# V turned by VectorE and stored in 128-byte runs, and one Strassen product added onto another's bank in the next quad

## The chip, the cores and the metric

One core of a Trainium2 chip runs the whole program. The metric is the device time of one execution in microseconds (us); the median of the runs counts. The engines are named as the profile names them: PE (TensorE, matrix products), PEld (its weight loads), DVE (VectorE), ACT (ScalarE), POOL (GpSimd) and SP (SyncE, which here issues nearly all DMAs, strictly in the order of the program).

## The reference

A decoder block of 2048 positions and width 1024, in float32. One combined projection feeds two branches:

```python
proj = x @ w_in[l] + b_in[l]                      # (2048, 1024) @ (1024, 9216)
q, k, v, g_attn, u_lru, g_lru, gate_logits = jnp.split(proj, SPLIT_POINTS, axis=-1)
...                                               # rotary q and k, three dilated band attentions
attn = jnp.sum(wts[..., None] * jnp.stack(outs, axis=0), axis=0)
attn = attn.reshape(B, S, ATTN_OUT_WIDTH).astype(dt) * jax.nn.silu(g_attn)
y_a = attn @ w_attn_proj[l]
...                                               # convolution, gated linear recurrence -> h
y_b = (h * jax.nn.silu(g_lru)) @ w_lru_proj[l]
merged = gates[:, :, 0] * y_a + gates[:, :, 1] * y_b
out = merged @ w_out[l] + b_out[l]
x = layer_norm(DEEPNORM_ALPHA * x + out, ln_gain[l], ln_bias[l])
```

The projection's 9216 columns are 72 tiles of 128: 12 each of q, k and v, 4 of the attention gate, 8 each of the recurrence's input and gate, 16 of merge gates.

## The kernel before

The kernel has three stages. The first, about two thirds of the time, is the projection; the second the attention; the third the output projections and the norm. The change is in the first.

**Quads and products.** The first stage works in quads: two column tiles (f0, f1) of the weights against two chunks of 512 positions (c0, c1), once for each half of the sequence, so 36 quads per half and 72 in all (`plan`, line 556). Results lie with the feature on the partition and the position along the row. Each operand is split into a high and a low float32r part, and a product of 128x512 with depth 512 takes 4 x 3 = 12 matmuls (`product`, line 607). The first quad of a half is computed plainly with 8 products; all others by Strassen's scheme with seven products P1 to P7, whose weights (A11, A12, A22, S1 to S4) and position blocks (B11, B21, B22, T1 to T4) are sums of quarters. The order of the products is written out by hand on line 122: MID for 66 quads, EDGE and FIRST for the last and the second of a half.

**Ticks.** The program is written out tick by tick: one tick is one product on PE (12 matmuls), and `where` (line 926) lists the ticks. In each tick the main loop first issues the product; then come the events due in this tick (weight loads, sums and the preparation of high and low weight parts: lines 680 to 705), then the chains, then `evacuate` (line 633), which takes the product's PSUM bank and forms results. Weights of quad s are prepared from `t0` on, which is 4 ticks ahead of the quad in the first half and 3 in the second, where low parts are loaded again from DRAM (`load_lo`, line 284) that the first half has stored there (`wl_scr`).

**Strassen sums.** `evacuate` keeps running sums in SBUF: `e` is P1, `u2` = P1 - P6, `u3` = u2 + P7. After P5 DVE forms the result for (f1, c1) and then adds P5 to `u2` (the profile's `u<-u,q`), to which P3 is added at the end for (f0, c1). The results of f1 come out with their sign turned (`sgn` = -1), and each later step corrects that. Products use four PSUM banks of tag `q`; two are used for the transposes (`t`), two for the gates of the recurrence (`g`).

**Chains.** A result starts a chain, a generator that goes on by one step when the tick, a free slot of the 32 SBUF slots and the estimated budget of the engines allow it (`run_chains`, line 187). `qk_chain` (line 299) does the rotation; it copies its tile with rows exchanged by four DMAs (`sw<-y`), and for the third dilation group stores q in runs of 128 bytes (line 341). `silu_chain` (line 398) makes the gates. `v_chain` (line 351) brings V to DRAM with the position on the row, as the attention reads it: PE turns the tile in four transposes of 128x128 into a PSUM bank (`vtp`, line 358), in the middle of a product; ACT copies the bank to one of two tiles `vs` and corrects the sign (line 366); and SP stores it with one DMA of 256 KB in runs of 512 bytes (line 370). There are 12 V tiles and 4 chunks, so 48 such chains; their transposes lie between 105 and 382 us and between 819 and 1100 us.

Of the kernel before, what the change touches and what calls it, by code (L numbers as in the profile page):

```python
# [31 lines left out]
def hybrid_block_kernel(ctx: ExitStack, tc: tile.TileContext, a: dict, out: bass.AP):  # L32
# [315 lines left out]
    vs_free = [sl_p.tile([P, 4, P], F32, name=f"vs{j}") for j in range(2)]  # L348
    tog = {"n": 0}

    def v_chain(vt, sgn, f, c):
        g, hp = divmod(f - FT_V, 4)
        st = {}

        def turn():
            tp = st["tp"] = ps.tile([P, 4, P], F32, tag="t", name=f"vtp{f}_{c}", bufs=2)
            for b in range(4):
                pe.transpose(tp[:, b, :], flat(vt)[:, b * P:(b + 1) * P], ident)  # L358
            give(vt)

        yield Ask(cond=lambda: tog["n"] < 2)
        tog["n"] += 1
        pe_later(2, turn)
        yield Ask(lag=3, cond=lambda: len(vs_free) > 0, ACT=.66)
        vs = vs_free.pop(0)
        act.activation(vs, st["tp"], AF.Copy, scale=sgn)
        tog["n"] -= 1
        yield Ask()
        dst = v_scr[g][hp // 2][c * CH:(c + 1) * CH, (hp % 2) * P:(hp % 2) * P + P]
        sp.dma_start(dst.rearrange("(b p) f -> p b f", p=P), vs)  # L370
        vs_free.append(vs)
# [26 lines left out]
    def silu_chain(y, sgn, f, c):  # L398
# [3 lines left out]
        act.activation(y, y, AF.Identity, scale=0.25 * sgn, bias=bq[:, f:f + 1])  # L402
# [157 lines left out]
    ticks = [8 if pl[2] is None else 7 for pl in plan]  # L560
    base = [sum(ticks[:s]) for s in range(NQ + 1)]
# [45 lines left out]
    def product(s, j):  # L607
# [6 lines left out]
        if first:  # L614
            Q["b"] = ps.tile([P, CH], F32, tag="q", name=f"q{j}_{s}", bufs=4)
        bank = Q["b"]
        h, l = U[s, n]
        i = 0
        for kk in range(4):
            ks = slice(kk * P, (kk + 1) * P)  # L620
            for w, xx in ((h, 0), (h, 1), (l, 0)):
                pe.matmul(bank, w[:, ks], x[:, kk, xx], start=(first and i == 0), stop=(last and i == 11))  # L622
                i += 1
            if i == 6:
                run(pe_late)
# [7 lines left out]
    def evacuate(s, j):  # L633
        half, _, order, _, _ = plan[s]
        b = Q["b"]
        c0, c1 = 2 * half, 2 * half + 1
        if order is None:
            fi, k, c = PLAIN[j]
            if k:
                result(s, fi, c0 + c, b, None)  # L640
            return
        pid = order[j]
        if pid == 1:
# [10 lines left out]
        elif pid == 5:  # L654
            result(s, 1, c1, b, Q["u3"])
            tt(dve, Q["u2"], Q["u2"], b, ALU.add)
# [3 lines left out]
        elif pid == 4:  # L660
            result(s, 1, c0, b, Q["u3"])
        elif order.index(5) > j:
            Q["p3"] = take(f"p{s}", F32)
            act.activation(Q["p3"], b, AF.Copy)
        else:
            result(s, 0, c1, b, Q["u2"])
        last = {"e": (2, 6), "u2": (3, 5), "u3": (4, 5), "p3": (5,)}
        for n, p in last.items():
            if n in Q and pid in p and all(order.index(x) <= j for x in p):
# [3 lines left out]
    COST = {1: dict(ACT=.66), 2: dict(DVE=.72), 6: dict(DVE=.72), 7: dict(DVE=.72), 5: dict(DVE=1.45), 4: dict(DVE=.72), 3: dict(DVE=.72)}  # L673
# [7 lines left out]
    for s in range(1, NQ):  # L681
# [20 lines left out]
        for j in range(7):  # L702
            if plan[s][0] and j % 2 == 0:
                at(t0 + j - 1, lambda s=s, j=j: load_lo(s, j))
            at(t0 + j, lambda s=s, j=j: prep_w(s, j))
# [220 lines left out]
    where = [(s, j) for s in range(NQ) for j in range(ticks[s])]  # L926
    for T, (s, j) in enumerate(where):
# [10 lines left out]
        if s == NQ - 1:  # L938
            for fn in ((), first[:2], first[2:], second[:2], firstv, second[2:], ())[j]:
# [652 lines left out]
```

## Time and profile before

| | |
|---|---|
| runs, us | 2103.63, 2104.59, 2108.65; median 2104.59 |
| profiled execution: its span, first to last instruction | 2101.9 us (its own device time isn't listed beside it) |
| PE busy | 2086.3 us, 99% of the span |
| DVE, ACT, POOL busy | 1662.7, 1116.7, 493.1 us |
| mean granted TensorE clock | 0.999 |
| first stage | to about 1440 us |
| time of DMA packets on the queue of SP (q1) | 70.5% of 16 engines |

The profile is of one execution. "Busy" is the time in which an engine had an instruction of a group running; matmuls are pipelined, so that their rows overlap, and a busy PE need not be PE at its peak. A row of a group gives line, engine and operation, out<-in, the tiles' shapes and the count, then busy time, mean ns of one, and the idle time ahead of it with what ended it. In a row of a stretch (from:to) stand the length, the busy time of each engine with its number of instructions, the granted clock, and the DMA engines' share and GB/s. SPq is SP's queue of DMA issues; the time of an issue is SP's own, and "to landing" goes from the issue until the data has arrived.

### The profile page before, as it was taken

Reading aid. Unit: us, or ns where it says so; the run is one execution under the profiler, and the core shown is the slowest. Engines: PE = TensorE matmul, PEld = TensorE weight load, DVE = VectorE, ACT = ScalarE, POOL = GpSimd, SP = SyncE. Lnnn points to the kernel's source line nnn. Section 1 sums busy time; section 2 is a strip of 40 time slices with the busy share of each in tenths; the row PEclk is TensorE's granted clock in tenths of the full one; section 3 lists DMA queues with packets and bytes.
Section 4 is the critical chain, followed back from the end, with each engine's and each line's share of the span. In section 5 each row is a group of like instructions: output and inputs, shape, how many; then the busy total and the mean of one; then the engine's idle time right before and its main releaser. Section 6 shows DMA issues by size and latency. Waiting matters only on the chain.

```text
span 2101.9 us, 35814 instructions
## 1 busy us (share of the span) xinstructions
PE 2086.3 (99%) x12016; PEld 1726.9 (82%) x12016; DVE 1662.7 (79%) x3179; ACT 1116.7 (53%) x2341; POOL 493.1 (23%) x468
## 2 busy tenths in 40 slices
PE   8999999999999999999999999999999999999998
PEld 7888888888888888888888888888999888888887
DVE  8987888889988867787877888877999645576667
ACT  6455456457457565666666775766999411211100
POOL 1111111110111011231221222222545344431120
PEclk9999999999999999999999999999999999999999
DMA  8987997987997967777779778769996788864432
GB/s 271 276 261 225 274 285 216 282 283 235 278 294 242 332 208 204 231 227 220 225 254 278 254 252 266 252 219 374 355 359 236 228 296 281 298 224 160 154 105 71
DMA packets 327160, 524.69 MB, mean 250 GB/s; under 512 B 105536, under 2 KB 135232, under 8 KB 323136
## 3 DMA queue, kind: packets, MB, share of 16 engines
q1 hardware_dynamic: 307088, 489.54, 70.5%
q0 software_dynamic: 12256, 19.42, 5.5%
q10 hardware_dynamic: 7632, 13.44, 1.7%
q8 instruction: 96, 1.57, 0.3%
q14 instruction: 88, 0.72, 0.1%
HBM read 317.14 MB, written 190.45 MB: 241 GB/s over the span
## 4 chain that ended last, share of the span: by engine, by line
PE 91%; DVE 3%; DMA 3%; ACT 2%; issue 1%; SPq 0%; DVEq 0%; ACTq 0%
PE q L622 66%; PE yb L1340 3%; PE yb L1341 3%; PE z L1451 3%; PE yb L1342 3%; PE z L1450 3%; PE z L1452 3%; ACT p L1023 2%; DVE p L1015 2%; PE ya L1419 1%; PE ya L1418 1%; PE ya L1420 1%; PE g L492 1%; PE vtp L358 1%; DMA B<-k_scr 1%; DMA o_scr<-ot 1%
## 5 line engine op out<-in xcount | busy, mean ns | idle before, releaser
L622 PE MATMUL q<-xT,hS 128*128 128x512 f32 x1680 | 521.0, 391 | 0.0
L622 PE MATMUL q<-xT,l 128*128 128x512 f32 x1120 | 436.0, 389 | 0.0
L622 PE MATMUL q<-xB,hA 128*128 128x512 f32 x1248 | 388.9, 393 | 6.0 <-ACT xB L215 6.0
L622 PEld LDWEIGHTS q<-xT,hS 128*128 128x128 f32 x1680 | 312.9, 188 | 69.0 <-issue 5.5
L622 PE MATMUL q<-xB,l 128*128 128x512 f32 x904 | 352.9, 390 | 0.0
L622 PEld LDWEIGHTS q<-xB,hA 128*128 128x128 f32 x1248 | 233.8, 189 | 57.3 <-ACT xB L215 6.0
L622 PEld LDWEIGHTS q<-xT,l 128*128 128x128 f32 x1120 | 210.2, 188 | 44.1
L622 PEld LDWEIGHTS q<-xB,l 128*128 128x128 f32 x904 | 170.3, 188 | 36.0
L245 POOL DMA_DIRECT2D wS<-in_w_in_dram x70 | 61.9, 950 | 491.5 <-DMA wS<-in_w_in_dram 140.0
L622 PE MATMUL q<-xB,hS 128*128 128x512 f32 x560 | 174.0, 392 | 0.0
L1023 ACT ACTIVATE p<-p,sta 128x256 f32<-128x256 f32 (+1 forms) x384 | 172.7, 469 | 1.2 <-PE pt L1034 0.8
L622 PE MATMUL q<-xT,hA 128*128 128x512 f32 x560 | 173.0, 390 | 0.0
L269 ACT ACTIVATE hA<-wA 128x512 fp32r<-128x512 f32 x218 | 134.9, 623 | 54.4 <-DMA wA<-in_w_in_dram 24.9
L269 ACT ACTIVATE hS<-S 128x512 fp32r<-128x512 f32 x175 | 109.0, 623 | 79.3 <-DVE S L227 49.0
L227 POOL TENSOR_TENSOR S<-S,wA 128x512 f32<-128x512 f32 x35 | 45.5, 1301 | 391.8 <-DVE S L227 208.8
L622 PEld LDWEIGHTS q<-xT,hA 128*128 128x128 f32 x560 | 104.7, 188 | 23.0 <-issue 1.5
L622 PEld LDWEIGHTS q<-xB,hS 128*128 128x128 f32 x560 | 104.0, 188 | 22.4 <-issue 1.5
L1015 DVE CUSTOM_DVE_ANT_0 p<-s,mask 128x256 f32<-128x256 f32 (+1 forms) x384 | 116.4, 360 | 0.2 <-PE s L1008 0.2
L1451 PE MATMUL z<-wo,mh 128*128 128x512 f32 (+1 forms) x264 | 101.0, 383 | 0.0
L1452 PE MATMUL z<-wo,ml 128*128 128x512 f32 (+1 forms) x264 | 101.0, 383 | 0.0
L1450 PE MATMUL z<-wo,mh 128*128 128x512 f32 (+1 forms) x264 | 101.0, 383 | 0.0
L227 DVE TENSOR_TENSOR l<-wA,hA 128x512 fp32r<-128x512 f32 x113 | 79.3, 702 | 26.9 <-ACT hA L269 26.6
(204 smaller groups left out, 4257.0 us busy)
## 6 DMA issues: line engine op xcount, KB each, us to landing
wA<-in_w_in_dram SPq DMA_DIRECT2D x253, 256.0 KB, 4.7
wl_scr<-l SPq DMA_DIRECT2D x105, 512.0 KB, 5.2
l<-wl_scr SPq DMA_DIRECT2D x105, 512.0 KB, 4.6
sw<-y SPq DMA_DIRECT2D x384, 64.0 KB, 3.2
wS<-in_w_in_dram SPq DMA_DIRECT2D x70, 256.0 KB, 4.8
wS<-in_w_in_dram POOLq DMA_DIRECT2D x70, 256.0 KB, 6.3
qh_scr<-hi SPq DMA_DIRECT2D x48, 256.0 KB, 5.5
v_scr<-vs SPq DMA_DIRECT2D x48, 256.0 KB, 4.4
```

The source lines that it names most:

```text
L227: eng.tensor_tensor(out=out, in0=in0, in1=in1, op=op)
L245: pool.dma_start(t, w_part(s, x), accum_op=ALU.add)
L269: act.activation(h, r, AF.Copy)
L622: pe.matmul(bank, w[:, ks], x[:, kk, xx], start=(first and i == 0), stop=(last and i == 11))
L1015: dve.tensor_tensor_reduce(out=st["p", i, j][:, h, lo:256], in0=st["s", i, j // 2][h][:, j % 2, lo:256], in1=mask[:, lo:256], scale=1.0, s ...
L1023: act.activation(p, p, AF.Exp, scale=-1.0, bias=s[:, h:h + 1], accum_out=s[:, 2 + h:3 + h])
L1340: pe.matmul(yb, WL[f][:, 0, k], xx[:, 0], start=(k == 0), stop=False)
L1341: pe.matmul(yb, WL[f][:, 0, k], xx[:, 1], start=False, stop=False)
L1342: pe.matmul(yb, WL[f][:, 1, k], xx[:, 0], start=False, stop=(k == 7))
L1450: pe.matmul(z, mh[:, k], w[:, 0, hs], start=(k == 0), stop=False)
L1451: pe.matmul(z, mh[:, k], w[:, 1, hs], start=False, stop=False)
L1452: pe.matmul(z, ml[:, k], w[:, 0, hs], start=False, stop=(k == 7))
```

## The change

*V chains.* The four transposes on PE, their PSUM bank and ACT's copy are gone. DVE turns the tile in blocks of 32x32 into a slot of its own, and SP stores it with four DMAs, one for each group of 32 partitions, in runs of 128 bytes, two in one tick and two in a later one. The sign of odd tiles is no longer corrected here: V stays negated there, and the attention gate of the same tiles is negated too.

*P3.* In MID quads P5 gets a bank of its own pair (`q5`, in place of the two banks of the transposes), and P3 is added onto that bank by PE itself. P3 is issued as the third tick of the next quad, so a MID quad has six ticks of its own and one of the quad before. Its weights' preparation moves by three ticks. DVE's add of P5 to `u2` is gone in these quads; `u2` is kept until P3 is done.

```diff
     def v_chain(vt, sgn, f, c):
         g, hp = divmod(f - FT_V, 4)
-        st = {}
-
-        def turn():
-            tp = st["tp"] = ps.tile([P, 4, P], F32, tag="t", name=f"vtp{f}_{c}", bufs=2)
-            for b in range(4):
-                pe.transpose(tp[:, b, :], flat(vt)[:, b * P:(b + 1) * P], ident)
-            give(vt)
-
-        yield Ask(cond=lambda: tog["n"] < 2)
-        tog["n"] += 1
-        pe_later(2, turn)
-        yield Ask(lag=3, cond=lambda: len(vs_free) > 0, ACT=.66)
-        vs = vs_free.pop(0)
-        act.activation(vs, st["tp"], AF.Copy, scale=sgn)
-        tog["n"] -= 1
-        yield Ask()
-        dst = v_scr[g][hp // 2][c * CH:(c + 1) * CH, (hp % 2) * P:(hp % 2) * P + P]
-        sp.dma_start(dst.rearrange("(b p) f -> p b f", p=P), vs)
-        vs_free.append(vs)
+        yield Ask(need=1, DVE=.72)
+        vs = take(f"vs{f}_{c}", F32)
+        dve.transpose(vs, flat(vt))
+        give(vt)
+        dst = v_scr[g][hp // 2][c * CH:(c + 1) * CH].rearrange("(b i) f -> i b f", i=32)
+        for a in range(4):
+            if a % 2 == 0:
+                yield Ask()
+            f0 = (hp % 2) * P + 32 * a
+            sp.dma_start(dst[:, :, f0:f0 + 32], vs[32 * a:32 * a + 32].rearrange("p (b f) -> p b f", f=32))
+        give_sent(vs)
...
-        act.activation(y, y, AF.Identity, scale=0.25 * sgn, bias=bq[:, f:f + 1])
+        act.activation(y, y, AF.Identity, scale=0.25 * (sgn if f >= FT_U else 1.0), bias=bq[:, f:f + 1])
...
-    ticks = [8 if pl[2] is None else 7 for pl in plan]
-    base = [sum(ticks[:s]) for s in range(NQ + 1)]
+    where = []
+    for s, pl in enumerate(plan):
+        own = [(s, j) for j in range(8 if pl[2] is None else 6 if pl[2] is MID else 7)]
+        where += own[:2] + ([(s - 1, 6)] if s and plan[s - 1][2] is MID else []) + own[2:]
+    base = [where.index((s, 0)) for s in range(NQ)] + [len(where)]
...
+        onto = order is MID and order[j] == 3
+        if order is MID and order[j] == 5:
+            Q[s, "p5"] = ps.tile([P, CH], F32, tag="q5", name=f"q{j}_{s}", bufs=2)
+        elif first and not onto:
             Q["b"] = ps.tile([P, CH], F32, tag="q", name=f"q{j}_{s}", bufs=4)
-        bank = Q["b"]
+        bank = Q[s, "p5"] if order is MID and order[j] in (5, 3) else Q["b"]
...
-                pe.matmul(bank, w[:, ks], x[:, kk, xx], start=(first and i == 0), stop=(last and i == 11))
+                pe.matmul(bank, w[:, ks], x[:, kk, xx], start=(first and i == 0 and not onto), stop=(last and i == 11),
+                          skip_group_check=onto)
...
         elif pid == 5:
             result(s, 1, c1, b, Q["u3"])
-            tt(dve, Q["u2"], Q["u2"], b, ALU.add)
+            if order is MID:
+                Q[s, "u2"] = Q.pop("u2")
+            else:
+                tt(dve, Q["u2"], Q["u2"], b, ALU.add)
...
+        elif order is MID:
+            u2 = Q.pop((s, "u2"))
+            result(s, 0, c1, b, u2)
+            give(u2)
+            return
...
         for j in range(7):
+            d = 3 if j == 6 and plan[s][2] is MID else 0
             if plan[s][0] and j % 2 == 0:
-                at(t0 + j - 1, lambda s=s, j=j: load_lo(s, j))
-            at(t0 + j, lambda s=s, j=j: prep_w(s, j))
+                at(t0 + j - 1 + d, lambda s=s, j=j: load_lo(s, j))
+            at(t0 + j + d, lambda s=s, j=j: prep_w(s, j))
...
+        bo = bq[:, FT_GA:FT_U].rearrange("p (j e) -> p j e", e=2)[:, :, 1]
+        dve.tensor_scalar(out=bo, in0=bo, scalar1=-1.0, scalar2=None, op0=ALU.mult)
```

More of the change, by code (lines that the diff above doesn't have):

```diff
@@ L345, in qk_chain @@
         give_sent(hi, rp)
-    vs_free = [sl_p.tile([P, 4, P], F32, name=f"vs{j}") for j in range(2)]
-    tog = {"n": 0}
     def v_chain(vt, sgn, f, c):
         g, hp = divmod(f - FT_V, 4)
-        st = {}
-        def turn():
-            tp = st["tp"] = ps.tile([P, 4, P], F32, tag="t", name=f"vtp{f}_{c}", bufs=2)
-            for b in range(4):
-                pe.transpose(tp[:, b, :], flat(vt)[:, b * P:(b + 1) * P], ident)
-            give(vt)
-        yield Ask(cond=lambda: tog["n"] < 2)
-        tog["n"] += 1
-        pe_later(2, turn)
-        yield Ask(lag=3, cond=lambda: len(vs_free) > 0, ACT=.66)
-        vs = vs_free.pop(0)
-        act.activation(vs, st["tp"], AF.Copy, scale=sgn)
-        tog["n"] -= 1
-        yield Ask()
-        dst = v_scr[g][hp // 2][c * CH:(c + 1) * CH, (hp % 2) * P:(hp % 2) * P + P]
-        sp.dma_start(dst.rearrange("(b p) f -> p b f", p=P), vs)
-        vs_free.append(vs)
+        yield Ask(need=1, DVE=.72)
[9 more added lines that the diff above has]
+        give_sent(vs)
     def store_chain(t, dst):
@@ L613, in product @@
             n, x, first, last, end = UNIT[order[j]], XB[BLK[order[j]]], True, True, True
-        if first:
+        onto = order is MID and order[j] == 3
+        if order is MID and order[j] == 5:
+            Q[s, "p5"] = ps.tile([P, CH], F32, tag="q5", name=f"q{j}_{s}", bufs=2)
+        elif first and not onto:
             Q["b"] = ps.tile([P, CH], F32, tag="q", name=f"q{j}_{s}", bufs=4)
-        bank = Q["b"]
+        bank = Q[s, "p5"] if order is MID and order[j] in (5, 3) else Q["b"]
         h, l = U[s, n]
@@ L634, in evacuate @@
         half, _, order, _, _ = plan[s]
-        b = Q["b"]
         c0, c1 = 2 * half, 2 * half + 1
@@ L639, in evacuate @@
             if k:
-                result(s, fi, c0 + c, b, None)
+                result(s, fi, c0 + c, Q["b"], None)
             return
         pid = order[j]
+        b = Q[s, "p5"] if order is MID and pid in (5, 3) else Q["b"]
         if pid == 1:
@@ L668, in evacuate @@
         for n, p in last.items():
+            if order is MID and n == "u2":
+                continue
             if n in Q and pid in p and all(order.index(x) <= j for x in p):
@@ L672, in hybrid_block_kernel @@
     Q = {}
-    COST = {1: dict(ACT=.66), 2: dict(DVE=.72), 6: dict(DVE=.72), 7: dict(DVE=.72), 5: dict(DVE=1.45), 4: dict(DVE=.72), 3: dict(DVE=.72)}
+    COST = {1: dict(ACT=.66), 2: dict(DVE=.72), 6: dict(DVE=.72), 7: dict(DVE=.72), 5: dict(DVE=.72), 4: dict(DVE=.72), 3: dict(DVE=.72)}
     events = {}
@@ L925, in hybrid_block_kernel @@
     low = NS
-    where = [(s, j) for s in range(NQ) for j in range(ticks[s])]
     for T, (s, j) in enumerate(where):
@@ L937, in hybrid_block_kernel @@
         run_chains()
-        if s == NQ - 1:
-            for fn in ((), first[:2], first[2:], second[:2], firstv, second[2:], ())[j]:
+        if T >= base[NQ - 1]:
+            for fn in ((), first[:2], first[2:], (), second[:2], firstv, second[2:], ())[T - base[NQ - 1]]:
                 fn()
```

## Prediction

> **What bounds the kernel now.** I read the page's first part, then the view of waits for PE, then the busy time of each engine by stretch, cut where the V transposes begin and end.
>
> ```profile
> span 2101.9 us, 35814 instructions
> PE 2086.3 (99%) x12016; PEld 1726.9 (82%) x12016; DVE 1662.7 (79%) x3179; ACT 1116.7 (53%) x2341; POOL 493.1 (23%) x468
> ```
> ```profile
> PE q L622 <- ACT xB L215: 6.0, 1, 6.0
> PE s L1008 <- DVE sta L1015: 0.5, 2, 0.3
> ```
> ```profile
> core 0: us, PE busy (x) PEld busy (x) DVE busy (x) ACT busy (x) POOL busy (x), PEclk, DMA share, GB/s
> 100.00:424.00 324.00, 324.00 (x1484) 265.49 (x1483) 270.38 (x424) 164.88 (x275) 44.26 (x54) 1.00 0.87 258
> 424.00:780.00 356.00, 356.00 (x1580) 291.25 (x1579) 307.66 (x478) 208.39 (x342) 45.97 (x54) 1.00 0.86 269
> 780.00:1102.00 322.00, 322.00 (x1478) 262.13 (x1477) 251.52 (x348) 200.15 (x326) 76.41 (x66) 1.00 0.74 226
> 1102.00:1400.00 298.00, 298.00 (x1327) 241.65 (x1326) 238.93 (x335) 200.42 (x320) 73.54 (x60) 1.00 0.81 255
> ```
>
> The reader is to see that PE is busy 1300.00 of the 1300 us from 100 to 1400, at a granted clock of 1.00, and that in the first stage it waited once, 6.0 us, at the very start. A busy PE alone proves little, since its ends are modelled; so I look at the pace. The next rows are PE's order of time around two bursts of the transposes that the change removes (start, duration).
>
> ```profile
> 380.65 0.62 PE L622 MATMUL q<-xT,hS 128*128 128x512 f32 x2
> 381.11 0.39 PE L622 MATMUL q<-xT,l 128*128 128x512 f32 x1
> 381.34 0.60 PE L358 MATMUL vtp<-ident,y 128*128 128x128 f32 x4
> 381.69 0.71 PE L622 MATMUL q<-xT,hS 128*128 128x512 f32 x2
> 382.24 0.40 PE L622 MATMUL q<-xT,l 128*128 128x512 f32 x1
> 382.47 0.62 PE L622 MATMUL q<-xT,hS 128*128 128x512 f32 x2
> 382.93 0.39 PE L622 MATMUL q<-xT,l 128*128 128x512 f32 x1
> ```
>
> Three products take 0.69 us from 382.24 to 382.93, so 0.23 us each. From 381.11 to 382.24 the same three and four transposes take 1.13 us: a burst costs PE 0.44 us, and the products close up around it. The stage runs at PE's own issue pace, and what is taken from PE's list shortens it, as long as no other resource then comes last.
>
> **The change, part by part.**
>
> *Transposes off PE.* 48 chains (12 V tiles, 4 token chunks) lose one burst each. The next rows are the same stretches as above, for the products (q), the transposes (vtp) and the gate products (g) alone; the column after the stretch's length is PE.
>
> ```profile
> 424.00:780.00 356.00, 350.21 (x1538) 287.81 (x1537) 82.58 (x121) 13.31 (x22) 1.00 0.86 269
> 780.00:1102.00 322.00, 309.47 (x1328) 246.56 (x1327) 77.63 (x111) 9.42 (x16) 1.00 0.74 226
> 1102.00:1400.00 298.00, 289.75 (x1267) 236.80 (x1266) 72.33 (x106) 8.77 (x15) 1.00 0.81 255
> ```
> ```profile
> 780.00:1102.00 322.00, 14.36 (x96) 11.88 (x96) 13.31 (x23) 1.00 0.74 226
> ```
> ```profile
> 424.00:780.00 356.00, 6.76 (x42) 3.44 (x42) 17.78 (x27) 1.00 0.86 269
> 780.00:1102.00 322.00, 8.68 (x54) 4.37 (x54) 25.91 (x38) 1.00 0.74 226
> 1102.00:1400.00 298.00, 9.65 (x60) 4.85 (x60) 26.84 (x40) 1.00 0.81 255
> ```
>
> The two stretches without transposes give two equations: 1538a + 42b = 356 and 1267a + 60b = 298, so a = 0.2264 us per product and b = 0.186 us per gate product. The stretch with half of the transposes then leaves 322 - 1328a - 54b = 322 - 300.6 - 10.0 = 11.3 us for 24 bursts, 0.47 us each. The timeline said 0.44, and the busy time of the 96 transposes, 14.36 us, gives 0.60 as an upper bound, since it counts overlap. I take 0.46: **48 x 0.46 = 22.1 us off PE**, between 21.1 and 28.7.
>
> *Transposes onto DVE, P3 off DVE.* DVE gets 48 transposes of 128x512 f32, which no row shows. The nearest rows are a one-source copy of the same shape and the add that writes through a permuted view:
>
> ```profile
> L1049 DVE COPY ptb<-pt 128x512 f32<-128x512 f32 x66 | 43.8, 683 | 0.1
> L227 DVE TENSOR_TENSOR rp<-y,sw 128x512 f32<-128x512 f32 x64 | 74.3, 1166 | 0.4
> L227 DVE TENSOR_TENSOR u<-u,q 128x512 f32<-128x512 f32 x70 | 47.4, 676 | 0.0
> L366 ACT ACTIVATE vs<-vtp 128x512 f32<-128x512 f32 x48 | 27.6, 589 | 30.4 <-DMA v_scr<-vs 14.1 <-PE vtp L358 12.4 <-PE q L622 3.9
> ```
>
> So 0.68 to 1.17 us each; I take 0.70, by the copy, since a transpose too reads one tensor and writes as many elements: 48 x 0.70 = 33.6 us more. Against it, 66 of the 70 `u<-u,q` adds (the MID quads) go, since P3 lands on P5's bank and one add serves both: 66 x 0.676 = 44.6 us. DVE is 11 us lighter in all, ACT 48 x 0.589 = 28 us. Neither is on PE's path. Inside 100 to 424, which holds some 16 quads (84 products, 19.0 us, and the bursts), DVE goes from 270.4 by +16.8 and -10.8 to 276 of a shortened 313 us, 88%; at 1.17 us per transpose, 92%. The next row shows DVE at 96% for 50 us with PE still at 50.00, so this cover holds:
>
> ```profile
> 450.00:500.00 50.00, 50.00 (x223) 40.92 (x222) 47.99 (x77) 28.43 (x52) 6.95 (x9) 1.00 0.86 278
> ```
>
> *P3 issued in the next quad.* The same twelve products with the same operands, as many ticks in all (66 quads give one to their successor), its weights S3 prepared three ticks later and so as far ahead as before; the other products of a quad from the third on get one tick more ahead. The bank of P5 is held until the third tick of the next quad, and gets a pair of its own in place of the two banks of the transposes, so `q` keeps its four for five products. The row for the cost of adding onto a filled bank is every product itself: eleven of its twelve matmuls already do it at 0.23 us. Zero; if the moved S3 came late, PE would wait, but its load and preparation move with it. The extra sign flip of the biases is one small DVE op at the start, under 0.2 us.
>
> *The stores.* This is the cost that can undo the gain. SP issues four DMAs of 64 KB per chain, each of 512 runs of 128 bytes, in place of one of 256 KB in 512 runs of 512 bytes. Behind SP's issues stand the weights of the next quads, the `sw` copies of the rotary chains and the low parts. SP's issue rows (min, median, max in ns):
>
> ```profile
> L370 SPq DMA_DIRECT2D v_scr<-vs x48: 365/384/1181, 106.6 to 1105.0; - x48
> L341 SPq DMA_DIRECT2D qh_scr<-hi x16: 524/577/1058, 77.1 to 1293.7; - x16
> L341 SPq DMA_DIRECT2D ql_scr<-rp x16: 2115/2678/5558, 77.8 to 1294.4; - x16
> L307 SPq DMA_DIRECT2D sw<-y x384: 507/588/1542, 61.5 to 1390.1; - x192
> DMA to landing us min/median/max: 4.2/5.7/11.1
> ```
>
> The second and third are already what the change adds: stores of 2048 runs of 128 bytes, of the third dilation group. One alone issues in 0.58 us; a second right behind it takes 2.7, as if it had to wait for room in the queue. The last line is their landing. A 64 KB DMA of 32 partitions (`sw<-y`) issues in 0.59. So a chain costs SP 4 x 0.59 = 2.4 us, against 0.4: +2.0 us. Upper bound, with the queue backed up, from the worst such pair:
>
> ```profile
> 410.81 1.06 SPq L341 DMA_DIRECT2D qh_scr<-hi  x1
> 411.96 5.56 SPq L341 DMA_DIRECT2D ql_scr<-rp  x1
> 417.61 3.53 SPq L330 DMA_DIRECT2D k_scr<-rp  x1
> 421.19 0.42 SPq L234 DMA_DIRECT2D wA<-in_w_in_dram  x1
> ```
>
> 410.81 to 421.19 is 10.4 us for 4096 runs and one plain store, so (10.4 - 0.4) / 2 = 5.0 us per 2048 runs: +4.6 us per chain. How much room is there? SP's order of time from 105 to 424 has 207 rows, of which these are the first and the last; their durations, overlaps counted once, make 236 us.
>
> ```profile
> 105.60 0.32 SPq L282 DMA_DIRECT2D wl_scr<-l  x1
> 423.83 0.67 SPq L234 DMA_DIRECT2D wA<-in_w_in_dram  x1
> ```
>
> With 24 chains that becomes 236 + 48 = 284 of 308 us at my price, and 236 + 110 = 346 at the upper one. From 780 to 1102 the same count is 193 (173 rows): 241 or 303 of 311. I take the low price: a chain's runs come in two pairs a tick (2.7 us) apart, four chains spread over some seven ticks, while the g2 pair throws 4096 at once. And the jam of 411 to 421 stopped SP for 10 us without a gap on PE. In the first half weights are loaded three to six ticks ahead of their preparation and prepared four ticks ahead of their product (lines 684 to 705), some 20 us in all, and a few us of lateness disappear in that. Cost on the path: 0, with 0 to 8 us as bounds.
>
> [...]
>
> **Sum.** The median of the runs is 2104.59, 2.7 us above the profiled span, which I carry over. 2104.6 - 22.1 + 0.2 + 0 = **2083 us** (rounded up from 2082.7), 1.0% less. The measurement of this kernel can tell about 0.3% (6.3 us) from no change. With the bounds of the terms: 2076 to 2091.
>
> **The rivals.**
>
> 1. *SP's queue becomes the bound, slower than before.* If 2048 short runs cost SP as in the worst pair, the first half's V quads need 346 us of SP in 308, and PE waits for up to the rest, 38 us: 2121, or 2103 if the lead of 20 us is still whole and catches what it can. It begins to decide at (308 - 236) / 24 + 0.4 = 3.4 us per chain in the first half; the gain is gone from 22 us of waits, (308 + 22 - 236) / 24 + 0.4 = 4.3 us per chain without the lead. For it: DMA share 0.87 there, the 5.56 us issue. Against it: spread over ticks, 0.59 us for a like DMA, and the second half has room even at the worst price. Chance 0.09. [...]
>
> 2. *The gain does not arrive.* Something that PE's 100% hides, such as weights arriving just in time, sets the pace of the V quads, and PE's freed time turns into waits: 2102 to 2105. Against it: the quads from 424 to 780 run without bursts at a = 0.2264 with more DVE load (86% against 83%) and the same DMA share. Chance 0.07.
>
> 3. *DVE comes late for the banks.* A transpose of 1.17 us or more, in order before an evacuation, lets the four `q` banks fill; longest idle of PE per V quad 1 us: 2083 + 12 = 2095. For it: DVE's 83% here. Against it: the 96% row. Chance 0.04.
>
> Forecast 0.80.
>
> **How the numbers follow.** Faster by over 0.3% (below 2098.3): forecast and rival 3, 0.84. Same: rival 2, 0.07. Slower: rival 1, 0.09. The range's low end takes 0.56 us per burst, most of the way to the overlap-counted 0.60; its high end reaches over the 8 us of stalls and rival 3 to stalls of some 17 us: 2078 to 2100. Left out are rivals 1 and 2 (0.16) and a little of each end.
>
> **What would show it.** Right: no `vtp` rows; PE 22 us less busy with 192 matmuls fewer, and still busy all of the first stage; `u<-u,q` at 4; DVE transposes near 700 ns; 192 `v_scr` issues near 0.6 us. Wrong: new PE waits on ACT `hA` or `hS` behind DMA `wA` (rival 1, with `v_scr` issues of 1 us and more), on DVE (rival 3), or a product pace above 0.2264 us (rival 2). My forecast is wrong if the first stage is shortened by less than 14 us.

## The result, and the profile after

The changed kernel takes 2123.18 us (median of 4 runs, 2121.19 to 2129.17), beside 2104.2 us for the kernel before (4 runs, 2103.63 to 2108.65): 1.0092 times as long, with an interval of 1.0079 to 1.0106. It is slower by 0.9%, where 1.0% faster was forecast. The profiled execution has a device time of 2121.19 us, 1.7 us above its span.

First the page's first part:

```profile
span 2119.5 us, 35477 instructions
PE 2077.4 (98%) x11824; PEld 1713.8 (81%) x11824; DVE 1678.4 (79%) x3162; ACT 1093.7 (52%) x2293; POOL 500.9 (24%) x468
```

PE's 192 transposes are gone (12016 - 11824), and the span is 17.6 us longer. The view of waits for PE (total us, times, longest) shows six kinds in the first stage where before there was one, `xB` at the start:

```profile
PE q L617 <- DMA l<-wl_scr: 8.1, 2, 5.8
PE q L617 <- DVE l L227: 7.2, 5, 2.5
PE g L481 <- DVE vl L227: 6.1, 2, 3.1
PE q L617 <- ACT xB L215: 5.8, 1, 5.8
PE q L617 <- ACT hA L269: 3.8, 1, 3.8
PE q L617 <- DVE u L227: 1.3, 2, 0.6
```

The busy times by stretch, for the same four stretches as before, tell where; the column after the stretch's length is PE, the third from the end the granted clock:

```profile
100.00:424.00 324.00, 312.56 (x1353) 253.12 (x1352) 267.81 (x421) 149.42 (x243) 42.48 (x52) 0.98 0.90 248
424.00:780.00 356.00, 352.99 (x1552) 288.57 (x1551) 303.30 (x469) 208.70 (x347) 45.48 (x54) 0.99 0.87 272
780.00:1102.00 322.00, 319.70 (x1422) 259.29 (x1421) 259.56 (x347) 191.92 (x307) 81.82 (x66) 1.00 0.80 225
1102.00:1400.00 298.00, 288.38 (x1274) 232.75 (x1273) 243.15 (x320) 194.58 (x313) 71.73 (x57) 0.98 0.82 250
```

PE, which was busy for all 1300 us, now stands still for 26 of them, and its clock is below 1.00 in three stretches. The same view in steps of 50 us puts nearly all of it into four of them:

```profile
200.00:250.00 50.00, 46.60 (x197) 37.49 (x197) 37.16 (x60) 11.72 (x21) 5.63 (x8) 0.97 0.90 242
250.00:300.00 50.00, 46.86 (x201) 37.93 (x200) 40.76 (x64) 26.89 (x44) 8.70 (x11) 0.97 0.96 256
400.00:450.00 50.00, 42.08 (x160) 32.45 (x159) 37.07 (x58) 24.24 (x41) 3.52 (x4) 0.86 0.91 261
1100.00:1150.00 50.00, 40.38 (x170) 32.00 (x169) 38.28 (x50) 22.90 (x36) 11.23 (x8) 0.90 0.78 206
```

DVE is no fuller there than elsewhere (74% from 200 to 250), so it is not the bound; it waits too. What for, the order of time from 214 to 239 shows (start, duration, engine, line; rows of PE and most of DVE left out):

```profile
214.34 1.30 DVE L352 STREAM_TRANSPOSE vs<-y 128x512 f32<-128x512 f32 x2
...
215.17 3.85 SPq L359 DMA_DIRECT2D v_scr<-vs  x4
...
217.39 1.30 DVE L352 STREAM_TRANSPOSE vs<-y 128x512 f32<-128x512 f32 x2
...
221.49 10.15 SPq L359 DMA_DIRECT2D v_scr<-vs  x12
...
231.74 2.41 SPq L307 DMA_DIRECT2D sw<-y  x4
...
235.72 0.69 DVE L227 TENSOR_TENSOR y<-y,cos 128x512 f32<-128x512 f32 x1 [11.48 <-DMA sw<-y]
...
238.20 0.63 ACT L335 ACTIVATE hi<-rp 128x512 fp32r<-128x512 f32 x1 [12.57 <-DMA wl_scr<-l]
```

All four transposes of this V quad stand within 4.4 us. After four of their stores, twelve stand in a row on SP and hold it for 10.15 us, 0.85 each, where the median of all 192 is 0.506 (the row of the tile; min, median, max in ns):

```profile
L359 SPq DMA_DIRECT2D v_scr<-vs x192: 302/506/4524, 105.3 to 1136.8; - x192
```

Behind them, in SP's order, stand the `sw` copies of the next rotation. DVE stands for 11.48 us at one product (`y<-y,cos`, which overwrites the tile that the copies read), without a row of its own from 224.24 to 235.72, and everything behind that in the program waits with it: evacuations of PE's banks, sums and low parts of weights. From 390.14 twelve stores hold SP for 9.62 us, and DVE then stands 11.76 us; at 1121 to 1137 groups of six and eight stores hold SP for 7.60 and 4.61 us, ACT and DVE wait 8.3 and 9.0 us for weights (`wA`) and PE 5.8 us for the low parts (`l`).

Twelve stores in a row don't always do this. The longest such hold of the same run passes without a gap:

```profile
1055.10 11.25 SPq L359 DMA_DIRECT2D v_scr<-vs  x12
```

PE was busy for all of the 20 us from 1050 to 1070. Where the stores stand matters, and not only how many come together.

The pace suffers as well as the waits. In steps of 5 us:

```profile
240.00:245.00 5.00, 2.01 (x8) 1.05 (x6) 5.00 (x8) 0.63 (x1) 0.00 (x0) 0.99 0.85 260
245.00:250.00 5.00, 4.80 (x15) 3.83 (x16) 4.21 (x8) 0.86 (x3) 0.00 (x0) 0.67 0.97 244
...
1135.00:1140.00 5.00, 0.86 (x2) 0.30 (x2) 4.97 (x6) 3.87 (x7) 2.94 (x2) 0.58 0.90 143
1140.00:1145.00 5.00, 3.00 (x7) 2.42 (x8) 4.83 (x7) 4.92 (x7) 1.40 (x1) 0.50 0.82 269
1145.00:1150.00 5.00, 5.00 (x21) 4.03 (x21) 4.83 (x8) 2.71 (x5) 0.01 (x1) 0.89 0.86 170
```

After two gaps of 0.64 and 2.55 us, with two products between them, PE's granted clock is 0.67 for the next 5 us; after gaps of 3.83 and 5.79 us it is at 0.50. PE's order of time shows the same: from 245.79 three products take 1.28 us, where 0.69 is the usual, and the usual pace is back some 3.2 us after the gap (4.0 us after the one that ends at 1142.00). Not every gap did this: PE stood for 1.75 us up to 406.79 and for 2.29 us up to 973.79, and the clock from 405 to 410 and from 973 to 978 is 1.00.

### The profile page after: what moved, and what is told of

It is laid out like the page before. It is cut to its first block, busy times and chain, and to the rows that moved or that the text cites. A ratio compares the mean times of both kernels' runs of the same rounds, so it can differ in the third digit from the quotient of the medians.

```text
span 2119.5 us, 35477 instructions
## 1 busy us (share of the span) xinstructions
PE 2077.4 (98%) x11824; PEld 1713.8 (81%) x11824; DVE 1678.4 (79%) x3162; ACT 1093.7 (52%) x2293; POOL 500.9 (24%) x468
## 4 chain that ended last, share of the span: by engine, by line
PE 75%; DMA 7%; DVE 6%; SPq 5%; ACT 5%; issue 2%; DVEq 0%; ACTq 0%
PE q L617 49%; ACT p L1031 3%; PE yb L1348 3%; PE yb L1349 3%; PE z L1460 3%; PE yb L1350 3%; PE z L1458 3%; PE z L1459 3%; SPq L359 2%; PE o L1072 2%; SPq L307 2%; PE s L1016 2%; PE ya L1428 1%; PE ya L1426 1%; PE ya L1427 1%
## 5 line engine op out<-in xcount | busy, mean ns | idle before, releaser
L227 DVE TENSOR_TENSOR y<-y,cos 128x512 f32<-128x512 f32 x96 | 81.0, 848 | 59.1 <-DMA sw<-y 59.0
L227 POOL TENSOR_TENSOR sw<-sw,sin 128x512 f32<-128x512 f32 x48 | 80.3, 1681 | 92.2 <-DMA sw<-y 61.7
L1459 PE MATMUL z<-wo,mh 128*128 128x512 f32 (+1 forms) x264 | 101.0, 383 | 0.0
```

The source lines that it names most:

```text
L227: eng.tensor_tensor(out=out, in0=in0, in1=in1, op=op)
L1459: pe.matmul(z, mh[:, k], w[:, 1, hs], start=False, stop=False)
```

## The experiments

All times are medians; the ratio is to runs of the kernel before on the same chip. The theory at the start: the stores' issue on SP (their number, their short runs) makes everything behind late. Rivals: the planner's budget on DVE, which bunches the chains; the moved P3, which I had counted at nothing; and DVE being simply too full.

### How a chain stores: one or four, long or short runs

The kernels e1, e2, e8 and later e7 and e9 move the same bytes, but put parts of V in wrong places of its scratch. They show what a store costs and are no kernels to use.

**e1_one_long.** The whole change, but a chain stores with one DMA in runs of 512 bytes.

```diff
-        for a in range(4):
-            if a % 2 == 0:
-                yield Ask()
-            f0 = (hp % 2) * P + 32 * a
-            sp.dma_start(dst[:, :, f0:f0 + 32], vs[32 * a:32 * a + 32].rearrange("p (b f) -> p b f", f=32))
+        yield Ask()
+        dst = v_scr[g][hp // 2][c * CH:(c + 1) * CH, (hp % 2) * P:(hp % 2) * P + P]
+        sp.dma_start(dst.rearrange("(b p) f -> p b f", p=P), vs.rearrange("p (b f) -> p b f", f=P))
```

> One store of 256 KB in runs of 512 bytes per V chain in place of four in runs of 128; DVE's transposes and the moved P3 stay. The 32x32 blocks land in the wrong places of V's scratch, so the attention's values are wrong; the bytes and everything after it are the same. Theory A (SP's queue: bunches of short-run stores hold up the sw copies and the weights behind them, DVE and ACT wait in order, PE stalls and then runs at a lower granted clock): no PE waits in the first stage after the start, granted clock 1.00 throughout, 2083 us. Theory B (the moved P3 makes PE wait for late preparations): still about 2120. Theory C (DVE's transposes, in order ahead of evacuations, hold up PE): still about 2120.

2094.89 us, 0.9952 (0.9937 to 0.9967): 28 us less than the change, and 12 above the 2083 expected. The stores alone decide over the sign, and something is left beside them.

**e2_four_long.** Four stores of 64 KB from 32 partitions each, as in the change, in runs of 512 bytes.

```diff
+        dst = v_scr[g][hp // 2][c * CH:(c + 1) * CH, (hp % 2) * P:(hp % 2) * P + P].rearrange("(b p) f -> p b f", p=P)
...
-            f0 = (hp % 2) * P + 32 * a
-            sp.dma_start(dst[:, :, f0:f0 + 32], vs[32 * a:32 * a + 32].rearrange("p (b f) -> p b f", f=32))
+            sp.dma_start(dst[32 * a:32 * a + 32], vs[32 * a:32 * a + 32].rearrange("p (b f) -> p b f", f=P))
```

> Four stores per V chain, as now 64 KB from 32 partitions each, two and two a tick apart, but in runs of 512 bytes (blocks land in the wrong places of V's scratch, so the attention's values are wrong). It parts the number of issues from the length of the runs. Theory A1 (the short runs fill the queue): issues near 0.5 us, none of 2 us and more, no PE stalls, 2083 to 2088. Theory A2 (four issues in place of one, 0.5 to 0.6 us each, are what SP can't take): the same stalls, 2110 to 2123.

2108.67 us, 1.002 (1.0011 to 1.0029): 14 us above one store, 14 below four short ones, and so between what the two theories expected.

**e8_one_short.** One store per chain, of 256 KB in 2048 runs of 128 bytes.

```diff
-        for a in range(4):
...
-            sp.dma_start(dst[:, :, f0:f0 + 32], vs[32 * a:32 * a + 32].rearrange("p (b f) -> p b f", f=32))
+        yield Ask()
+        dst = v_scr[g][hp // 2][c * CH:(c + 1) * CH].rearrange("(p x) y -> p (x y)", p=P)
+        sp.dma_start(dst.rearrange("p (r h f) -> p r h f", h=2, f=32)[:, :, hp % 2], vs.rearrange("p (r f) -> p r f", f=32))
```

> The whole change, but one store of 256 KB per V chain, from all 128 partitions in 2048 runs of 128 bytes (runs land in the wrong places of V's scratch, so the attention's values are wrong). With the first two experiments it makes a square: one or four issues, long or short runs. If the number of issues and the short runs each cost on their own, as the first two suggest (14 us from one to four long ones, 14 us from four long to four short ones): 2106 to 2111. If only the number of runs that enter the queue counts: 2118 to 2125. If only the issues count: 2095.

2113.1 us, 1.0046 (1.0031 to 1.0061). The row of its store's issue (min, median, max in ns):

```profile
L357 SPq DMA_DIRECT2D v_scr<-vs x48: 513/582/6088, 104.2 to 1119.8; - x48
```

The median is the 0.58 of a lone `qh_scr` store, the longest is over ten times as much. The square is closed: one long 2094.9, four long 2108.7, one short 2113.1, four short 2123.2. Short runs cost 14 to 18 us and four stores in place of one 10 to 14; both halves of the edit matter.

### The rivals among the causes

**e3_no_budget.** The transpose asks for no share of DVE.

```diff
-        yield Ask(need=1, DVE=.72)
+        yield Ask(need=1)
```

> The transpose no longer waits until the planner sees room on DVE (Ask without DVE=.72), so each of the four chains of a V quad should store in its own ticks. Nothing else changes; same computation. Theory A with bunching as its point: the longest run of V stores on SP falls from 12 (10 us) to 6 or fewer, stalls mostly go, 2083 to 2095. If the sum of the queue's time counts and not the bunching: no gain, 2115 to 2125. If DVE's order is what hurts (theory C): slower than 2123, since the transposes now come ahead of other work.

2112.51 us, 1.0034 (1.0022 to 1.0047), 11 us less than the change and in none of the expected ranges. The longest run of V stores on SP fell from twelve to six, as was meant, and yet PE's gaps stay at 244, 267, 410 and 432. This placing of the chains is worth some 11 us; the bunch of twelve isn't the main cause.

**e10_v_spread.** In the kernel of e6 (below), at most one pair of V stores in a tick.

```diff
-                yield Ask()
+                yield Ask(cond=lambda: vcap["n"] != now["n"] or vcap["k"] < 1)
+                vcap["k"] = vcap["k"] + 1 if vcap["n"] == now["n"] else 1
+                vcap["n"] = now["n"]
```

> V chains as in e6 (2114.5 us; products and sums as before, 34 slots, four stores of 128-byte runs), but no more than one pair of V stores is issued in a tick, over all chains; same computation. Theory A with bunching as its point: no runs of V stores longer than 2 to 4 on SP, PE waits mostly gone, 2086 to 2096, faster than both kernels. If the queue's total time per V quad is what counts: 2108 to 2116.

2108.08 us, 1.0011 (1.0001 to 1.0021), against 2114.5 for e6. Now never more than four V stores stand in a row. Spreading helps by 6 us, and PE's gaps stay in the same places. Bunching by itself isn't the whole of it.

**e6_v_only.** The V part of the change alone: P3 stays where it was, with P5 added by DVE; 34 slots, as the two `vs` tiles are gone.

```diff
-    NS, NL = 32, 4
+    NS, NL = 34, 4
...
+        vs = take(f"vs{f}_{c}", F32)
+        dve.transpose(vs, flat(vt))
```

> The V chains as after (DVE turns, four stores of 128-byte runs by SP), the products and sums as before. 34 SBUF slots in place of 32, in the room of the two vs tiles. Theory A (the stores do nearly all of the harm): 2105 to 2115, the jams of V stores on SP and the PE waits behind them as in the whole change. Theory B (the moved P3 does a good part): 2090 or below.

2114.5 us, 1.0052 (1.0037 to 1.0067). The V part alone already ends slower than before, and has 31 of the 40 us by which the change lies above the forecast; the moved P3 isn't the main cause.

**e7_v_only_long.** The same with one long store per chain (the diff of e1 in the kernel of e6).

> As the run before it, but one store in runs of 512 bytes per chain (blocks land in the wrong places of V's scratch, so the attention's values are wrong); products and sums as before, 34 slots. If the 11 us that the first experiment left over come with the moved P3: no PE waits after the start, 2083 us. If they come with the V quads being shorter or with DVE's transposes: 2090 to 2096, as in the first experiment.

2086.01 us, 0.9911 (0.9895 to 0.9928): 3 us from the 2083 that I had forecast for the whole, though without the moved P3 and without the short runs. SP's order at the place where the change jammed:

```profile
219.94 0.38 SPq L357 DMA_DIRECT2D v_scr<-vs  x1
220.58 3.05 SPq L307 DMA_DIRECT2D sw<-y  x4
223.72 1.11 SPq L357 DMA_DIRECT2D v_scr<-vs  x2
224.95 4.53 SPq L307 DMA_DIRECT2D sw<-y  x4
```

The first `sw` copies are issued at 220.58, eleven microseconds sooner than in the change (231.74).

**e9_one_long34.** e1 with 34 slots, so that P3 is the only difference to e7.

> The first experiment (whole change, one store of long runs per chain, attention's values wrong) with 34 SBUF slots in place of 32. Against e7 (2086 us) it then differs by the moved P3 alone. If the 9 us between e1 (2095) and e7 are those of the moved P3: 2093 to 2097. If they are those of the scarce slots: 2084 to 2088.

2092.27 us, 0.9936 (0.9921 to 0.9951). Two more slots give 2.6 us (e1 to e9), and the moved P3 costs 6.3 here (e7 to e9).

**e5_p3_only.** P3 moved, the V chains as before. The two banks of the transposes are then taken, so `q` has three banks and `q5` one.

```diff
-            Q[s, "p5"] = ps.tile([P, CH], F32, tag="q5", name=f"q{j}_{s}", bufs=2)
+            Q[s, "p5"] = ps.tile([P, CH], F32, tag="q5", name=f"q{j}_{s}", bufs=1)
...
-            Q["b"] = ps.tile([P, CH], F32, tag="q", name=f"q{j}_{s}", bufs=4)
+            Q["b"] = ps.tile([P, CH], F32, tag="q", name=f"q{j}_{s}", bufs=3)
```

> The V chains as before (PE turns, ACT copies, one store of 512-byte runs), and the moved P3 as after. So that the banks fit, q has three banks and q5 one. Theory B (the moved P3 delays DVE or its operands, which is what is left of the stalls when the V stores are long): PE waits on DVE vl and DMA l in the first stage, 2110 to 2116, some 10 us above the kernel before. Theory B0 (the move is free and the rest comes with the faster V quads): no new PE waits, 2102 to 2106.

2140.79 us, 1.0177 (1.0162 to 1.0192), and this doesn't tell what it was meant to. PE waits for results that free a bank:

```profile
PE q L628 <- DVE y L571: 18.0, 13, 2.7
```

With one bank fewer for `q` such waits are to be expected, so P3's own price can't be read from it.

### Who issues, and what stands next to a V quad

**e4_act_queue.** The whole change, the V stores issued by ACT.

```diff
-            sp.dma_start(dst[:, :, f0:f0 + 32], vs[32 * a:32 * a + 32].rearrange("p (b f) -> p b f", f=32))
+            act.dma_start(dst[:, :, f0:f0 + 32], vs[32 * a:32 * a + 32].rearrange("p (b f) -> p b f", f=32))
```

> The four short-run stores are issued by ACT on its own queue, in the same ticks; same computation. Theory A (the place in SP's queue): sw and weights no longer stand behind them, PE stalls go, 2083 to 2092; ACT pays about 192 x 0.5 = 100 us of issuing in its 47% of idle time. If the DMA engines are short of time, and not SP's queue: sw and weights land late all the same, 2105 to 2125. If ACT, stopped by a full queue, holds up the weights' high parts: PE waits on ACT hA and hS, 2100 to 2130.

2141.69 us, 1.0174 (1.0159 to 1.0189), the worst of all. The view of waits for ACT:

```profile
ACT hS L269 <- DMA v_scr<-vs: 42.4, 7, 11.2
ACT e L641 <- DMA v_scr<-vs: 28.8, 4, 10.8
```

```profile
229.22 11.64 ACTq L359 DMA_DIRECT2D v_scr<-vs  x8
```

Eight stores take ACT's own queue of issues 11.64 us, and the `hS` behind them starts 11.2 us late. ACT prepares the high part of every weight, so PE waits in turn: 27.1 us for `hS` and `hA` together, where the change has 3.8.

**e11_v_pool.** e6 with the V stores issued by GpSimd (`pool.dma_start` in the same line).

> V chains as in e6, with the four short-run stores issued by POOL on its own queue, which the trace shows 12% busy in the first half; same computation. If what hurts is the place in SP's order, and POOL can issue 192 stores at about 1 us each (its DMA issues of wS take 0.95): 2085 to 2095. If the DMA engines are what the runs fill, wherever they are issued: 2105 to 2120. If POOL falls behind with its weight sums (S4, the accumulating wS loads): PE waits on hS, 2100 to 2130.

2101.76 us, 0.9983 (0.9973 to 0.9992): 12.7 us less than e6, and between the first two expectations.

**e12_v_half.** The even chunks turned by DVE and stored as in the change, the odd ones turned by PE and stored as before.

```diff
+            start_chain(qk_chain(y, f, c) if kind == "qk" else (v_chain_pe if c % 2 else v_chain_dve)(y, sgn, f, c))
```

> Half of the V chains (even chunks) go by DVE and four short-run stores, the other half by PE, ACT and one store, as before; products and sums as before; same computation. Half of the bursts, 11 us, leave PE. Theory A with a threshold (a jam hurts only beyond the lead of the weights and sw copies): 8 V stores in a row at most, almost no PE waits, 2093 to 2097. If the harm goes with the number of stores: half of e6's, 2109.

2109.19 us, 1.0018 (1.0008 to 1.0027). Half of the short stores still make gaps (3.6 us at 264 to 274, 3.9 at 1122 to 1134), while half of the bursts stay on PE.

In the change all 26 us of PE's gaps follow two of a half's six V quads, the third and the last; in e2, e3, e6 and e10 most of them do. These two stand directly ahead of a quad of the third dilation group, whose q goes out in runs of 128 bytes as well (`ql_scr`, L341). They also stand directly behind another q and k quad, where the other four stand behind a quad of the recurrence. Those four store the same runs in the change without a gap.

**e13_re_after.** The whole change, with the attention-gate quads put in the places of the third and the last V quad.

```diff
-    light += [("ga", FT_GA + 2 * j, FT_GA + 2 * j + 1) for j in range(2)] + mg[2:]
+    ga = [("ga", FT_GA + 2 * j, FT_GA + 2 * j + 1) for j in range(2)]
+    light = light[:2] + ga[:1] + light[2:4] + ga[1:] + light[4:] + mg[2:]
```

> The whole change, with the two V quads that stand right before a quad of the third dilation group exchanged with the two quads of the attention gate, so that no V quad is followed by one of the third group. Same computation. Theory A' (the V stores alone fit beside the rest; what PE pays for is their meeting the short-run stores and sw copies of the next third-group quad): the stalls at 240 to 272, 404 to 442, 970 and 1130 go, 2092 to 2102. Theory A (any bunch of V stores costs its share): stalls move with the V quads, 2115 to 2125.

2101.47 us, 0.998 (0.9971 to 0.9989): 22 us less than the change. The gaps at 240 to 245, at 404 to 414 and at 973 are gone. The one at 264 is not: it is 4.14 us, against 3.14 in the change. And with V stores twelve in a row, up to 10.56 us on SP (from 1041.87), PE is busy for all of the 35 us from 1035 to 1070.

**e14_re_v_only.** The same order in the kernel of e6.

> The V part alone (e6, 2114.5 us) with the same exchange of quads. Theory A': 2084 to 2094, faster than both kernels. Theory A: 2110 to 2118.

2105.84 us, 1.0004 (0.9995 to 1.0014): 9 us less than e6, and outside both expected ranges.

**e15_re_v_pool.** The same order in the kernel of e11.

> The V part alone with POOL issuing the stores (e11, 2101.8 us) and the same exchange. Theory A': 2083 to 2090. Theory A: 2100 to 2104.

2090.95 us, 0.9935 (0.9918 to 0.9952): the fastest of those that do the whole of the work. It beats the kernel before by 0.65% and the change by 1.5%.

**e16_re_before.** The control: the new order alone, in the kernel before.

> The kernel before with the exchange alone, as a control. PE is busy without a gap in its first stage with either order, so both theories: 2102 to 2107.

2114.24 us, 1.0045 (1.0029 to 1.006). The order is worse for the old kernel, by 9 us, which neither theory had expected; PE then waits at its own transposes:

```profile
PE vtp L358 <- DVE y L569: 4.4, 3, 2.9
```

So the new order isn't good in itself. It takes 22 us from the change and gives the old kernel 9. If the two simply add, the place of the V quads is worth some 31 us in the change; the same sum from e6 and e14 is 18 us, so its size isn't settled.

Nor is it settled which neighbour does it, since the exchange takes the two V quads away from the third group's quad behind them and from the q and k quad ahead of them, both at once. The trace of the change speaks for both. The first wait at each place comes before the third group stores anything: SP's twelve V stores end at 231.64, and the first short-run store of that group leaves at 242.45. The second gap comes behind such a store:

```profile
254.48 4.62 SPq L341 DMA_DIRECT2D ql_scr<-rp  x1
...
265.80 0.69 DVE L227 TENSOR_TENSOR S<-S,wA 128x512 f32<-128x512 f32 x1 [2.32 <-DMA wA<-in_w_in_dram]
```

SP issues this `wA` right behind, in 3.78 us from 259.16; DVE waits for it, and PE for DVE, 3.14 us. In the kernel before DVE waits for `wA` at the same place (3.11 us at 263.05), and PE has no gap.

**e17_after_pool.** The whole change in its own order, the V stores issued by GpSimd.

> The whole change as given; only the 192 V stores are issued by GpSimd's queue instead of SyncE's. Theory (SyncE is held by its own issues, 10.15 us for twelve in a row, so the sw copies and weights behind them come late): the long waits of DVE for sw (11.48 us) shrink below 6 us, PE's idle time in the first stage falls from 32.4 to about 18 us, and the time falls from 2123 to about 2105 (V part alone: 2114.5 to 2101.8, a fall of 12.7; here the loss is larger). Rival (the DMA engines' work on 128-byte runs delays everything behind, whoever issues it): 2118 or more, with waits for sw of 9 us and more staying.

2102.42 us, 0.9987 (0.9978 to 0.9997). The time came out near the 2105 expected, and PE's idle time at 20.5 us near the 18. The longest wait of DVE for `sw` fell to 6.6 us, not below 6, and their sum only from 59.0 to 53.6 us, so it is not the sum of these waits that costs. SP's order at the first jam:

```profile
221.79 3.90 SPq L307 DMA_DIRECT2D sw<-y  x4
```

The first copies leave at 221.79, nearly as early as in e7. But a second thing changed with the issuer. The page's line of packets, first for the change, then for e17, with the row of GpSimd's queue in each:

```profile
DMA packets 403191, 524.67 MB, mean 248 GB/s; under 512 B 206144, under 2 KB 211264, under 8 KB 399168
...
q0 software_dynamic: 12256, 19.42, 5.4%
```
```profile
DMA packets 307960, 524.68 MB, mean 250 GB/s; under 512 B 107840, under 2 KB 112960, under 8 KB 303936
...
q0 software_dynamic: 18400, 32.01, 8.5%
```

From SP the V stores were 98304 packets (192 x 512) of 128 bytes. From GpSimd the profile counts 6144 more on its queue for 12.59 MB, 2 KB each. So e17 shows that the issuer decides, not whether through SP's time or through the form of the transfer.

**e18_re_after_pool.** Both remedies in the whole change.

> The whole change, V stores issued by GpSimd, and the attention-gate quads swapped with the third and the last V quads of the first half and second half, so that no V quad stands directly before a third-group q and k quad. Theory (both causes are one, stores of short runs from two sources meeting in one queue): the two remedies overlap, so less than the sum of their gains; 2085 to 2095, no granted clock lost, PE idle in the first stage below 13 us. Rival (P3 moved costs 6 to 10 us of its own, whatever the queue): 2097 to 2101, slower than the V part alone with the same two remedies (2090.95).

2099.67 us, 0.9982 (0.9972 to 0.9991): hardly less than either alone, and 8.7 us above e15, which has both remedies but not the moved P3. The rival held, in this pair.

### The account

From slices of 1 us between 0 and 1450 come PE's idle time (what its busy time leaves of the slice) and the clock lost (its busy time in the slice times what the granted clock lacks to 1.00, so that no idle time is counted twice). The kernel before has 6.7 and 0 us. The last column is the change of the span less those two. All are of the profiled execution, which lies up to 4.3 us off the median.

| kernel | span against before | more PE idle | clock lost | rest |
|---|---|---|---|---|
| the change | +17.6 | +25.7 | 11.4 | -19.5 |
| e7, V alone, one long | -17.1 | +3.1 | 1.7 | -21.9 |
| e1, one long | -9.2 | +8.1 | 3.4 | -20.7 |
| e9, one long, 34 slots | -11.6 | +7.7 | 0.0 | -19.3 |
| e2, four long | +2.9 | +16.5 | 6.5 | -20.1 |
| e8, one short | +13.8 | +20.7 | 11.3 | -18.2 |
| e6, V alone | +9.6 | +22.5 | 4.7 | -17.6 |
| e10, V alone, spread | +5.6 | +16.7 | 6.9 | -18.0 |
| e3, no budget | +9.3 | +19.2 | 8.3 | -18.2 |
| e4, ACT issues | +37.9 | +39.6 | 11.9 | -13.6 |
| e13, order | -5.9 | +10.7 | 4.6 | -21.2 |
| e14, V alone, order | +3.4 | +16.4 | 1.7 | -14.7 |
| e11, V alone, GpSimd | -5.2 | +11.2 | 1.7 | -18.1 |
| e15, V alone, order, GpSimd | -11.1 | +8.4 | 0.0 | -19.5 |
| e17, GpSimd issues | -1.3 | +13.8 | 3.9 | -19.0 |
| e18, order, GpSimd | -7.2 | +8.6 | 4.9 | -20.7 |
| e12, half of the transposes | +3.7 | +7.8 | 4.7 | -8.8 |
| e5, P3 alone, transposes kept | +36.8 | +25.1 | 5.1 | +6.6 |
| e16, order, transposes kept | +10.1 | +6.1 | 1.7 | +2.3 |

The rest holds the transposes' own time, and whatever the later stages vary by. It is 17.6 to 21.9 us in fourteen kernels between 2086 and 2123 us; e14 and e4 have less, e12 about half. The two kernels that keep all transposes should have none, and have +2.3 and +6.6, so a row is good to some 7 us. Within that, taking the bursts off PE paid in every kernel; what differs is how much came back as gaps and as a lower clock.

## Why the prediction was wrong, point by point

*Bursts off PE: right.* 48 x 0.46 = 22.1 us was forecast; e7's rest is 21.9 and the change's 19.5.

*Transposes onto DVE: right in the price, wrong in the sum.* The groups after:

```profile
L352 DVE STREAM_TRANSPOSE vs<-y 128x512 f32<-128x512 f32 x48 | 32.1, 692 | 1.2 <-PE q L617 1.2
L227 DVE TENSOR_TENSOR u<-u,q 128x512 f32<-128x512 f32 x4 | 2.7, 680 | 0.0
L227 DVE TENSOR_TENSOR wA<-wA,wA 128x512 f32<-128x512 f32 x35 | 42.4, 1211 | 0.0
```

A transpose takes 0.69 us (0.70 forecast), and 66 of the 70 additions are gone. Yet DVE's busy time went up by 15.7 us, not down by 11: others of its operations became longer, the sum `wA<-wA,wA` most (27.9 us before, 42.4 now). That sum runs in the second half only, where PE's gaps in the change ended with `l` and `hA`, behind DMAs; it is not what PE waited for there.

*P3 moved at no cost: wrong, and its size isn't settled.* Pairs that differ in P3 (and, in all but the first, in 34 slots against 32, which were worth 2.6 us where tried) give it +6.3 (e9 against e7), +8.7 (the change against e6), +0.7 (e17 against e11), +8.7 (e18 against e15) and -4.4 us (e13 against e14). The kernels of a pair ran on different chips in part, whose times for the kernel before differ by 1.2 us at most. No fixed price does for these.

*The stores: this step failed.* "Cost on the path: 0, with 0 to 8 us as bounds." e1 against the change puts 28 us on them, of which 18 are PE's gaps and 8 the clock lost. Three of its reasons fell:

- "Four chains spread over some seven ticks": in the third and the last V quad of the first half all four transposes stand within 4.4 us (in the other four over 20 to 30), and the stores come as four and twelve. I took an even spread where a planner sets the dates. A chain took SP about 3 us on the average (the rows of all V stores together, some 141 us), where I had 2.4 and the median of 0.506 would give 2.0. But the bunch is only part of it: without it e3 still takes 2112.5 us, and the twelve from 1055.10 cost nothing.
- "The jam of 411 to 421 stopped SP for 10 us without a gap on PE": true, and the change has such holds without a gap as well. Whether a hold costs anything depends on its place, which e13 shows (22 us), and I had reckoned with the total of the stretch. The total was no problem: SP's rows from 105 to 413 make 256 us, less than the 284 of 308 that I had allowed. But in the 60 us from 200 to 260 they make 55 us, where they made 44 before.
- The lead of 20 us. It doesn't protect the `sw` copies, which are wanted within a few ticks, by an engine that stands still for them. DVE's waits for `sw` went from 16.1 us (9 of them) to 59.0, as the view of waits for DVE has it after the change:

```profile
DVE y L227 <- DMA sw<-y: 59.0, 24, 11.8
```

Nor did it protect the weights everywhere. Of PE's 26 us of gaps some 8 come behind the late `sw`, 6 behind a late `wA` in the first half (at 267 and 437), and 12 behind `hA` and `l` in the second half, for which I had checked only SP's total.

A term was missing beside these: the clock, which fell after some of the gaps (to 0.67 and 0.50 in the stretches above), 11 us by the account. I had priced a wait of PE as its own length.

*The rivals.* The first (SP's queue) names the place, at 0.09, and its 2121 is close, but by luck: it comes from a queue over-full on the average, 346 us in 308, and SP's rows make 256. (Its other figure should be 2101 and not 2103, as 38 us less a lead of 20 leaves 18.) The second (no gain arrives) is wrong, as the account shows the gain arriving everywhere. The third (DVE late for the banks) appears only as a consequence: DVE was late because it stood for `sw` and `wA`; its transposes take 0.69 us and not 1.17. The signs given at the end were mixed: the missing `vtp` rows, the transposes' price and the median of the issues pointed to right; the waits on `hA`, and PE's busy time, which fell by 8.9 us and not by 22, to wrong.

What stays open: which neighbour of the two V quads makes their stores costly; how GpSimd's issue helps (above); why P3's price changes its sign; why the new order costs the old kernel 9 us.

## What to carry to other kernels

Price a new DMA on an in-order queue place by place, and neither by its median nor by the total of a stage: ask which chains fall due together, which transfers already stand next to them, and which engine stops for the transfer behind. Twelve stores held SP for 10 us at one place and PE stood still; 11 us at another cost nothing. A copy that an engine waits for within a few ticks was the first to be late here, but the weights with their long lead were late too. And count a gap on PE together with the slower clock that may come after it: here another 11 us for 26 us of gaps, in e9 none for 7.7.

## What the runs showed of the hardware

*SP and ACT stood still while their stores were issued.* SP was held 10.15 us by twelve 64 KB stores, ACT 11.64 us by eight of its own (e4); GpSimd issued each in 0.651 us at the median and 1.411 at most (e15). The choice of the issuer was worth -21 us (GpSimd) or +19 us (ACT), while the time of the packets on the queues of SP and GpSimd together hardly differs: 77.9% of the DMA engines in the change, 77.1% in e17.

*DVE's sum `wA<-wA,wA` took longer beside GpSimd's `S<-S,wA`.* First two pairs from the order of time before, then one after:

```profile
1100.76 1.30 POOL L227 TENSOR_TENSOR S<-S,wA 128x512 f32<-128x512 f32 x1 [9.11 <-DVE S L227]
1102.07 0.68 DVE L227 TENSOR_TENSOR wA<-wA,wA 128x512 f32<-128x512 f32 x1
...
1181.73 1.29 POOL L227 TENSOR_TENSOR S<-S,wA 128x512 f32<-128x512 f32 x1 [5.76 <-DVE S L227]
1182.77 0.81 DVE L227 TENSOR_TENSOR wA<-wA,wA 128x512 f32<-128x512 f32 x1
```
```profile
1177.88 1.29 POOL L227 TENSOR_TENSOR S<-S,wA 128x512 f32<-128x512 f32 x1 [17.38 <-ACT si L390]
1178.17 1.55 DVE L227 TENSOR_TENSOR wA<-wA,wA 128x512 f32<-128x512 f32 x1
```

The kernel before and the change have 35 of these sums each. The 15 before and 6 after that no sum of GpSimd's overlaps take 0.68 to 0.69 us. The 20 before and 27 after that start within GpSimd's, 0.19 to 1.04 us ahead of its end, end 0.54 to 0.56 us after that end (1183.02 and 1179.17 in the rows above), however early they began. The two left, after the change, start 0.06 us ahead of its end and 0.04 us ahead of its start, and take 0.69 and 0.68 us. The mean of this sum lies between 1147 and 1251 ns in five kernels with the moved P3 (the change, e5, e13, e17, e18) and between 796 and 839 in three without it (before, e6, e15).
